# Two-layer attention and conv-FFN trunk on one core: gate and up products with the high and the low part of the tokens side by side in one 512 column operand

## The chip, the core and the metric

The kernel runs on one core of one Trainium2 chip. The metric is device microseconds of one execution, the median of three runs. The engines are named as the profile names them: PE (TensorE, matrix products; PEld is its load of the stationary operand), ACT (ScalarE), DVE (VectorE), POOL (GpSimd), and SP, whose queue issues the weight DMAs.

## What is computed

The reference is a decoder trunk of two layers over 256 tokens of width 1024: layer 0 mixes tokens by block attention (one block covers all 256 tokens here), layer 1 by differential attention. After each mixer comes the part that is changed here, a feed forward with a causal convolution of width 3 on its gate branch:

```python
def conv_ffn(x, w_in, conv_w, conv_b, w_out):
    h = x @ w_in                                             # (256, 1024) @ (1024, 2 * 2816)
    gate = causal_dwconv(h[..., :D_FF], conv_w, conv_b)      # 3 taps along the tokens
    return (jax.nn.silu(gate) * h[..., D_FF:]) @ w_out       # (256, 2816) @ (2816, 1024)

for i in range(DEPTH):                                       # DEPTH = 2
    h = h + mixer_i(rmsnorm(h, norm_mix_g[i]))
    h = h + conv_ffn(rmsnorm(h, norm_ffn_g[i]), ...)
```

All of it is float32. The kernel reaches that precision by splitting each factor of a product into a high part of type float32r and a low part, the rest, and summing three products: high by high, high by low, low by high.

## The kernel before

**Weights.** They come from HBM as 98 chunks of [128, 2048] (1 MB), in the order of their use, into the ring `raw` of 3 buffers. `split_next` (line 156) splits a chunk in two halves of 1024 columns: ACT copies the high part into `wh` (line 165), DVE subtracts to get the low part `wl` (line 167). Both have 5 buffers, so the split of chunk c + 5 waits until PE is through with chunk c. `split_upto` says how far the splits have got at each place of the program.

**Tokens.** The normalised activations lie with the features on the partitions in two tiles, `xh` (high) and `xl` (low), each [128, 2 token tiles, 8 contraction tiles, 128].

**Feed forward** (`ffn`, line 679). The 2816 hidden features go in 11 pairs of 128, j = 0 to 10. Each pair has three chunks: gate (u = 0), up (u = 1) and out (u = 2). Pair 0 is computed with the tokens on the partitions (`first_pair`) and turned by transposes (`turn`), since one tile of tokens is normalised before the other. Pairs 1 to 10 use `form_b` (line 697): for a gate or an up chunk, and for each of its two blocks b of 128 features, 3 x 8 products of 256 moving columns (all tokens) accumulate into one half of a PSUM bank:

```python
for ph in range(3):
    for k in range(KT):
        r.append(mm(p[:, b * 256:(b + 1) * 256], w[:, k, b], (xh, xh, xl)[ph][:, :, k], ...))
```

`post_gate` (line 710) takes the bank of the gate to SBUF: per block one ACT instruction with the last tap as scale and the bias (line 715), two DVE instructions for the other taps (line 717), and for the pair one Silu on ACT (line 719). `post_up` (line 722) multiplies that by the bank of the up product on DVE (line 724) and splits the result into a high part (ACT, line 726) and a low part (DVE, line 727) in the tile `arena`. `outp` (line 732) multiplies it by the out chunk, products of 512 columns into four accumulators `acc`.

**Order.** From the second pair on the loop asks, for j = 2 to 10, for gate(j), out(j - 2), up(j). After the last pair come out(9) and out(10), the sum with `h` and the next norm (`tail`, and `finish` at the end of the kernel). All PE work of 128 x 512 results uses two PSUM pools of four banks, `acc` and `wk`; `form_b`, the transposes and the scores use `wk`. The order of the instructions on ACT and DVE, and small moves on PE, are a scheduler's; the table `PLAN` places a few small works among the products (`turn`: after how many products the transposes of pair 0 stand).

In names such as wh22 the number is the chunk: 16 and 17 are gate and up of pair 0 in layer 0, 18 and 19 those of pair 1, 20 gate of pair 2, 21 out of pair 0, 22 up of pair 2, 23 gate of pair 3; 95 is up of pair 10 of layer 1, 96 and 97 are out of pairs 9 and 10.

Of the kernel before, what the change touches and what calls it, by code (L numbers as in the profile page):

```python
# [32 lines left out]

# the places of the small works among the products: slots of 24 products, or products
PLAN = {
# [21 lines left out]
    "norm_2": (42, 58),  # L57
    "turn": (21, 32),
}
# [3 lines left out]
def tile_trunk(  # L63
# [35 lines left out]

    # ---- inputs that come first  # L100
    h = [const.tile([128, D], F32, name=f"h{t}") for t in range(NT)]
# [21 lines left out]

    # ---- the stream of weight chunks, each split into two parts that sum to it
    raws, WH, WL = {}, {}, {}
# [23 lines left out]
    def after(engine):  # L149
        """the splits do not go before a chain that the products wait for"""  # L150
        return tc.issue_after(behind[engine].ins) if engine in behind else nullcontext()
# [21 lines left out]
    def split_upto(n):  # L173
        """n: pieces, two to a chunk (after the first)"""
        while state["split"] < min(n + 2, len(pieces)):
            split_next()

    def pump(c):
        """chunk c and those before it"""
        return [(PLAN["pump"][0], lambda: split_upto(2 * c + 1)), (PLAN["pump"][1], lambda: split_upto(2 * c + 2))]  # L180
# [37 lines left out]

    # ---- normalised activations, transposed and split
    xh = const.tile([128, NT, KT, 128], F32R, name="xh")  # L220
    xl = const.tile([128, NT, KT, 128], F32R, name="xl")
    st = {}
# [7 lines left out]
    def stats(t, i):  # L230
        """sum of squares over half i of the columns of h[t]"""
        junk = work.tile([128, D], F32, name="junk", bufs=1)[:, cols(i)]
        return nc.scalar.activation(junk, h[t][:, cols(i)], AF.Square, scale=1.0 / 32.0,
                             accum_out=st[t][1][:, i:i + 1])
# [30 lines left out]
    def gain_t(t, i, layer, parts=((0, 1, 2, 3),)):  # L265
        """without the scale of the norm, which the products get"""
        for ks in parts:
# [13 lines left out]

    # ---- matrix products: lists of single instructions, so that others go between
    def mm(o, l, r, start, stop):
# [3 lines left out]
    def passes(n, lh, ll, rh, rl):  # L287
        """(k, left, right) over the three products of parts"""
        return ([(k, lh, rh) for k in range(n)] + [(k, lh, rl) for k in range(n)]
                + [(k, ll, rh) for k in range(n)])  # L290

    def run(main, smalls=(), unit=1):
        """write down the products, with the small works at their places among them"""
        n = len(main)
        at = {}
        for pos, f in smalls:
            at.setdefault(min(pos * unit, n), []).append(f)
        for i in range(n + 1):
            for f in at.get(i, []):
                f()  # L300
            if i < n:
                main[i]()

    def proj(o, c0, t):
        """[128 tokens, 512] of the projection whose weights are chunks c0, c0 + 1"""
        r = []
        for c in (c0, c0 + 1):
            for k in (0, 2):
                r += proj_part(o, c, 4 * (c - c0), k, t, c == c0 and k == 0, c > c0 and k == 2)
        return r  # L310

    def proj_part(o, c, kt, k0, t, first, last):
        """the part of proj that comes from two rows of tiles of one chunk"""
        r = []
# [7 lines left out]

    # ---- attention
    def mixer(layer, base):
# [16 lines left out]
        def tables():  # L341
            """the rotary tables, times the scale of the norm"""
            p = wk()
# [6 lines left out]
        def evac_qk(p, kind, hf, j):  # L350
            """two heads, features on the partitions"""
            if j == 0:
# [132 lines left out]

        # where the small works go: (slot of 24 products, place in it)
        def ev(time, f, *a):
# [14 lines left out]

        # projections
        def form_b(o, c0, hl):
            """[128 features of a head, 256 tokens]"""
            r = []
# [76 lines left out]

        # the projection of the output
        b = base + 12
# [21 lines left out]
    def tail(m0, m1, po, gi=None):  # L607
        """the last products of a part, the sum with h and the norm that follows"""
        mix = gi is None
# [21 lines left out]
    def finish(outp, po, gi):  # L631
        """the last products, the sum with h and the last norm"""
        def products(t, n, *where):
# [43 lines left out]

    # ---- feed forward
    def ffn(layer, base):
# [16 lines left out]

        def form_b(j, u):
            p = wk()
            c = chunk_of[j, u]
            r = []  # L700
            for b in range(2):
                for ph in range(3):
                    for k in range(KT):
                        w = (WH, WL, WH)[ph][c].rearrange("p (k b f) -> p k b f", k=KT, b=2)
                        r.append(mm(p[:, b * 256:(b + 1) * 256], w[:, k, b],
                                    (xh, xh, xl)[ph][:, :, k],
                                    ph == 0 and k == 0, ph == 2 and k == KT - 1))
            return p, r

        def post_gate(j, p):  # L710
# [11 lines left out]
        def post_up(j, p):  # L722
            y = G[j]
            nc.vector.tensor_tensor(y, y, p.rearrange("p (b q) -> p b q", b=2), op=ALU.mult)  # L724
            g = arena([2, 2, 256], F32R)
            nc.scalar.copy(g[:, 0], y)  # L726
            nc.vector.tensor_tensor(g[:, 1], y, g[:, 0].bitcast(F32), op=ALU.subtract)
            G[j] = g
# [3 lines left out]
        def outp(j, t, n, o=None, off=0):  # L732
            """the part of pair j in [128 tokens, 512], or in 256 of its columns"""
            g = G[j]
# [15 lines left out]

        # the first pair with tokens on the partitions: one tile of them is ready before the other
        tok = {}
# [24 lines left out]
        split_upto(2 * (base + 5) + 2)  # L777
        p, r = form_b(1, 0)

        def both():  # L780
            turn(1)
            post_gate(0, pg)
            post_up(0, pu)

        run(r, [(PLAN["turn"][1], both)])
        post_gate(1, p)
        split_upto(2 * (base + 6) + 2)
        p, r = form_b(1, 1)
        run(r)
        post_up(1, p)  # L790
        for t in range(2):
            for n in range(2):
                po[t, n] = acc()
        for j in range(2, NP):
            for u in range(2):
                split_upto(2 * (chunk_of[j, u] + 3) + 2)
                p, r = form_b(j, u)
                run(r)
                (post_gate if u == 0 else post_up)(j, p)
                if u == 0:  # L800
# [12 lines left out]

    # ---- the whole
    fixed = tc.manual_schedule()
# [18 lines left out]
def ffn_order():  # L834
    """the order in which the feed forward asks for its chunks: (pair, gate | up | out)"""
    seq = [(0, 0), (0, 1), (1, 0), (1, 1)]
# [78 lines left out]
```

## Time and profile before

| | |
|---|---|
| median of 3 runs | 623.27 us (621.47 to 624.48) |
| profiled execution: span from the first to the last instruction | 620.5 us |
| median less that span (what lies around the instructions) | 2.8 us |
| mean granted TensorE clock | 0.997 |
| PE busy | 609.2 us, 98% |
| DVE, ACT busy | 410.3 us (66%), 345.6 us (56%) |
| HBM read | 104.58 MB, 170 GB/s over the span |

The profile gives no separate device time for the profiled execution; its span is what the sum is made against, and 2.8 us is added to compare with the median. A busy PE is not PE at its peak, since matmuls overlap; how long a product takes of PE is read from the distance between the starts of products that follow each other. Small groups of rows are merged: "x8" behind a row of the timeline says that eight like instructions stand in it.

### The profile page before, as it was taken

The numbers are of one execution on the slowest core, as the hardware profiler recorded it, in microseconds if no ns is written. First come the engines' busy times: TensorE is split into PE (matmuls) and PEld (weight loads), VectorE is DVE, ScalarE is ACT, GpSimd is POOL, SyncE is SP. The second block draws the span as 40 slices with busy tenths as digits, with TensorE's granted clock in tenths as the row PEclk, the third lists the DMA queues.
The fourth block names the chain that finished last, engine by engine and source line by source line (L and its number), as shares of the span: only waits on it lengthen the run. The fifth ranks groups of instructions, "written<-read, shape, count | busy, mean of one in ns | idle before, by whom it ended". The sixth has DMA issues, their size and how long they took to land.

```text
span 620.5 us, 10285 instructions
## 1 busy us (share of the span) xinstructions
PE 609.2 (98%) x4203; PEld 561.6 (91%) x4203; DVE 410.3 (66%) x676; ACT 345.6 (56%) x560; POOL 18.6 (3%) x29
## 2 busy tenths in 40 slices
PE   7999999999999999999999999999999999999996
PEld 5999988899999999999889998889999999999985
DVE  3799684587655665566575899965876566556624
ACT  5777574276454455445477798744755544444512
POOL 1100000000000000000010001011000000000000
PEclk9999999999999999999999999999999999999998
DMA  8686345165555455545353612450765545545101
GB/s 286 213 308 240 139 153 203 69 229 198 185 204 175 169 200 204 173 171 200 136 196 116 232 69 77 170 209 22 271 213 194 184 164 195 203 163 182 65 0 69
DMA packets 16756, 106.28 MB, mean 171 GB/s; under 512 B 2115, under 2 KB 2627, under 8 KB 4422
## 3 DMA queue, kind: packets, MB, share of 16 engines
q1 hardware_dynamic: 16422, 105.24, 47.8%
q8 instruction: 33, 0.54, 0.4%
q10 hardware_dynamic: 288, 0.39, 0.2%
q14 instruction: 13, 0.11, 0.0%
HBM read 104.58 MB, written 1.05 MB: 170 GB/s over the span
## 4 chain that ended last, share of the span: by engine, by line
PE 88%; ACT 5%; DMA 2%; DVE 2%; issue 1%; SPq 0%; POOL 0%; POOLq 0%; ACTq 0%
PE acc L284 46%; PE wk L284 37%; DMA raw<-in_wts_dram 2%; PE wk L383 2%; ACT swap L360 2%; ACT wh L165 1%; ACT sc L398 1%; DVE wl L167 1%; PE wk L424 1%; PE wk L257 1%; PE wk L480 0%; DVE swap L363 0%; DVE arena L364 0%; PE wk L443 0%; PE wk L442 0%
## 5 line engine op out<-in xcount | busy, mean ns | idle before, releaser
L167 DVE TENSOR_TENSOR wl<-raw,wh 128x1024 fp32r<-128x1024 f32 (+1 forms) x198 | 236.1, 1220 | 62.1 <-ACT wh L165 62.1
L165 ACT CAST wh<-raw 128x1024 fp32r<-128x1024 f32 (+1 forms) x198 | 198.2, 1040 | 94.3 <-PE wk L284 63.5
L284 PE MATMUL acc<-wh,arena 128*128 128x512 f32 x472 | 132.1, 397 | 0.0
L284 PEld LDWEIGHTS acc<-wh,arena 128*128 128x128 f32 x472 | 86.9, 188 | 19.4 <-ACT arena L726 0.5
L284 PE MATMUL wk<-xh,wl 128*128 128x256 f32 x640 | 90.0, 283 | 0.0
L284 PE MATMUL wk<-xl,wh 128*128 128x256 f32 x640 | 89.8, 283 | 0.0
L284 PE MATMUL wk<-xh,wh 128*128 128x256 f32 x640 | 89.4, 282 | 0.0
L284 PEld LDWEIGHTS wk<-xh,wh 128*128 128x128 f32 x640 | 83.4, 191 | 1.6
L284 PEld LDWEIGHTS wk<-xl,wh 128*128 128x128 f32 x640 | 82.6, 192 | 0.0
L284 PEld LDWEIGHTS wk<-xh,wl 128*128 128x128 f32 x640 | 82.5, 192 | 0.0
L284 PE MATMUL acc<-wl,arena 128*128 128x512 f32 x236 | 73.0, 398 | 0.0
L717 DVE SCALAR_TENSOR_TENSOR qsb<-wk,conv,qsb 128x255 f32<-128x255 f32 (+1 forms) x88 | 41.7, 480 | 40.7 <-ACT qsb L715 39.3
L715 ACT ACTIVATE qsb<-wk,conv 128x256 f32<-128x256 f32 x44 | 24.7, 563 | 58.6 <-PE wk L284 57.2
L284 PEld LDWEIGHTS acc<-wl,arena 128*128 128x128 f32 x236 | 44.0, 188 | 10.3
L724 DVE TENSOR_TENSOR qsb<-qsb,wk 128x512 f32<-128x512 f32 x22 | 15.0, 687 | 45.2 <-PE wk L284 44.2
L284 PE MATMUL acc<-xh,wh 128*128 128x256 f32 x256 | 43.0, 286 | 0.1
L284 PE MATMUL acc<-xh,wl 128*128 128x256 f32 x256 | 43.1, 285 | 0.0
L284 PE MATMUL acc<-xl,wh 128*128 128x256 f32 x256 | 41.5, 284 | 0.0
L284 PEld LDWEIGHTS acc<-xh,wh 128*128 128x128 f32 x256 | 35.7, 191 | 0.6 <-ACT wh L165 0.3
L284 PEld LDWEIGHTS acc<-xh,wl 128*128 128x128 f32 x256 | 35.7, 191 | 0.1
L284 PEld LDWEIGHTS acc<-xl,wh 128*128 128x128 f32 x256 | 35.3, 191 | 0.1
L360 ACT COPY swap<-acc 8x512 f32<-8x512 f32 (+1 forms) x48 | 27.7, 578 | 10.9 <-PE acc L284 8.8
(109 smaller groups left out, 553.5 us busy)
## 6 DMA issues: line engine op xcount, KB each, us to landing
raw<-in_wts_dram SPq DMA_DIRECT2D x96, 1024.0 KB, 4.8
h<-in_x_dram SPq DMA_DIRECT2D x4, 256.0 KB, 6.7
raw<-in_wts_dram SPq DMA_DIRECT2D x4, 256.0 KB, 6.1
raw<-in_wts_dram SPq DMA_DIRECT2D x2, 512.0 KB, 7.9
out_dram<-hn SPq DMA_DIRECT2D x2, 320.0 KB, 2.5
tab<-in_rope_dram SPq DMA_DIRECT2D x2, 256.0 KB, 6.8
out_dram<-hn ACTq DMA_DIRECT2D x2, 192.0 KB, 2.7
lamv<-in_lams_dram SPq DMA_DIRECT2D x1, 128.0 KB, 6.0
```

The lines of the kernel that those rows point to most:

```text
L165: nc.scalar.copy(hi, r)
L167: nc.vector.tensor_tensor(lo, r, hi.bitcast(F32), op=ALU.subtract)
L257: nc.tensor.transpose(p[:, k * 128:(k + 1) * 128], st[t][0][:, (4 * i + k) * 128:(4 * i + k + 1) * 128], ident)
L284: return lambda: nc.tensor.matmul(o, l() if callable(l) else l, r() if callable(r) else r, start=start, stop=stop)
L360: nc.scalar.copy(w[a:a + half], pv[b:b + half])
L383: nc.tensor.matmul(p[:, b * 128:(b + 1) * 128], q[r, hl, tq * 128:(tq + 1) * 128], k[r, hl, tk * 128:(tk + 1) * 128], start=True, stop=True)
L398: nc.scalar.activation(es[m][:, c], es[m][:, c], AF.Exp, bias=sm[:, 1, i:i + 1], scale=scale, accum_out=sm[:, 2, i:i + 1])
L424: nc.tensor.transpose(p[:, b * 128:(b + 1) * 128], es[0][:, b * 128:(b + 1) * 128], ident)
L715: nc.scalar.activation(y[:, b], pb, AF.Identity, bias=cw[:, 3:4], scale=cw[:, 2:3])
L717: nc.vector.scalar_tensor_tensor(y[:, b, s:], pb[:, :256 - s], cw[:, 2 - s:3 - s], y[:, b, s:], op0=ALU.mult, op1=ALU.add)
L724: nc.vector.tensor_tensor(y, y, p.rearrange("p (b q) -> p b q", b=2), op=ALU.mult)
```

## The change

Three things change, all in the feed forward's pairs 1 to 10 of both layers.

1. `xh` and `xl` become views of one tile `xx` [128, 8 contraction tiles, 2 parts, 2 token tiles, 128], so that for one contraction tile the high and the low part of all 256 tokens are 512 columns in a row.
2. `form_b` does one block of 128 features at a time, in a bank of its own. For each contraction tile there is one product of 512 columns (high weights by high and low tokens) and one of 256 columns (low weights by high tokens) that adds to the right half of the bank.
3. The two halves of the bank are summed on the way out (`summed`): ACT copies the left half to a tile `zg` or `zu`, DVE adds the right half. The convolution of the gate then reads that tile in SBUF, and its first tap goes from ACT to DVE. The product with the up branch waits for both blocks of `zu`.

The place of the second `turn` is now 16, the end of the first block.

```diff
-    "turn": (21, 32),
+    "turn": (21, 16),
...
-    xh = const.tile([128, NT, KT, 128], F32R, name="xh")
-    xl = const.tile([128, NT, KT, 128], F32R, name="xl")
+    xx = const.tile([128, KT, 2, NT, 128], F32R, name="xx")
+    xh = xx[:, :, 0].rearrange("p k t q -> p t k q")
+    xl = xx[:, :, 1].rearrange("p k t q -> p t k q")
...
-        def form_b(j, u):
+        def form_b(j, u, b):
             p = wk()
             c = chunk_of[j, u]
             r = []
-            for b in range(2):
-                for ph in range(3):
-                    for k in range(KT):
-                        w = (WH, WL, WH)[ph][c].rearrange("p (k b f) -> p k b f", k=KT, b=2)
-                        r.append(mm(p[:, b * 256:(b + 1) * 256], w[:, k, b],
-                                    (xh, xh, xl)[ph][:, :, k],
-                                    ph == 0 and k == 0, ph == 2 and k == KT - 1))
+            for k in range(KT):
+                hi, lo = (w[c].rearrange("p (k b f) -> p k b f", k=KT, b=2)[:, k, b] for w in (WH, WL))
+                r.append(mm(p, hi, xx[:, k].rearrange("p c t q -> p (c t q)"), k == 0, False))
+                r.append(mm(p[:, 256:], lo, xx[:, k, 0].rearrange("p t q -> p (t q)"), False, k == KT - 1))
             return p, r
+        def summed(name, b, p):
+            if b == 0:
+                parts[name] = work.tile([128, 2, 256], F32, name=name)
+            z = parts[name][:, b]
+            nc.scalar.copy(z, p[:, :256])
+            nc.vector.tensor_tensor(z, z, p[:, 256:], op=ALU.add)
+            return z
+        def gated(j, b, z):
+            if b == 0:
+                G[j] = work.tile([128, 2, 256], F32, name="qsb", bufs=3)
+            y = G[j]
+            cw = conv_t[:, layer, 2 * j + b]
+            nc.vector.tensor_scalar(y[:, b], z, cw[:, 2:3], cw[:, 3:4], op0=ALU.mult, op1=ALU.add)
+            for s in (1, 2):
+                nc.vector.scalar_tensor_tensor(y[:, b, s:], z[:, :256 - s], cw[:, 2 - s:3 - s],
+                                               y[:, b, s:], op0=ALU.mult, op1=ALU.add)
+            if b == 1:
+                nc.scalar.activation(y, y, AF.Silu)
+        def part_done(j, u, b, p):
+            z = summed(("zg", "zu")[u], b, p)
+            if u == 0:
+                gated(j, b, z)
+            elif b == 1:
+                post_up(j, parts["zu"])
...
-                p, r = form_b(j, u)
-                run(r)
-                (post_gate if u == 0 else post_up)(j, p)
+                for b in range(2):
+                    p, r = form_b(j, u, b)
+                    run(r)
+                    part_done(j, u, b, p)
```

Pair 0 keeps `post_gate` and its way through `turn`. The mixers' products are as before, but read the new tile.

How the instructions stand now, at the places that the prediction speaks of. **PE, one gate chunk** (names: result <- moving, stationary or the other way round; the number behind a tile's name is its buffer). Before, pair 3 of layer 0, both blocks into one bank:

```order
L284 MATMUL wk_2019<-xh_109,wh29_1853 128x256 x8
L284 MATMUL wk_2019<-xh_109,wl29_1854 128x256 x8
L284 MATMUL wk_2019<-xl_110,wh29_1853 128x256 x8
L284 MATMUL wk_2019<-xh_109,wh29_1853 128x256 x8
L284 MATMUL wk_2019<-xh_109,wl29_1854 128x256 x8
```

Now, the end of the second block of a gate chunk (pair 2) and the first products of the out chunk that follows:

```order
L285 MATMUL wk_1548<-xx_109,wh20_1323 128x512
L285 MATMUL wk_1548<-xx_109,wl20_1324 128x256
L285 MATMUL wk_1548<-xx_109,wh20_1323 128x512
L285 MATMUL wk_1548<-xx_109,wl20_1324 128x256
L285 MATMUL wk_1548<-xx_109,wh20_1323 128x512
L285 MATMUL wk_1548<-xx_109,wl20_1324 128x256
L285 MATMUL acc_1512<-wh21_1390,arena_1428 128x512 x2
```

The 24 products of a block, in three runs of 8, became 16 that change width and stationary operand at every step.

**ACT at the start of the first feed forward**, from the copy that leads to the second `turn`. Before:

```order
L771 COPY qsb_1389<-acc_1336 128x512
L165 CAST wh22_1472<-raw22_1322 128x1024 x2
L715 ACTIVATE qsb_1436<-wk_1332,conv_104 128x256
L715 ACTIVATE qsb_1464<-wk_1399,conv_104 128x256
L165 CAST wh23_1537<-raw23_1330 128x1024
L715 ACTIVATE qsb_1436<-wk_1332,conv_104 128x256
L715 ACTIVATE qsb_1464<-wk_1399,conv_104 128x256
```

Now:

```order
L801 COPY qsb_1388<-acc_1335 128x512
L165 CAST wh22_1461<-raw22_1321 128x1024
L745 ACTIVATE qsb_1419<-wk_1331,conv_104 128x256
L715 COPY zg_1431<-wk_1398 128x256
L165 CAST wh22_1461<-raw22_1321 128x1024
L165 CAST wh23_1516<-raw23_1329 128x1024
L745 ACTIVATE qsb_1419<-wk_1331,conv_104 128x256
L715 COPY zg_1431<-wk_1438 128x256
```

Pair 0's gate lies in the bank wk_1331 (before wk_1332); its second block's instruction (L745, before L715) stands behind the first half of chunk 23 in both, but that bank is now the next one that PE asks for: the second up block of pair 1 goes into it. DVE's share of the same stretch, now:

```order
L747 SCALAR_TENSOR_TENSOR qsb_1419<-wk_1331,conv_104,qsb_1419 128x255
L728 SCALAR_TENSOR_TENSOR qsb_1434<-zg_1431,conv_104,qsb_1434 128x255
L747 SCALAR_TENSOR_TENSOR qsb_1419<-wk_1331,conv_104,qsb_1419 128x254
L728 SCALAR_TENSOR_TENSOR qsb_1434<-zg_1431,conv_104,qsb_1434 128x254
L716 TENSOR_TENSOR zg_1431<-zg_1431,wk_1438 128x256
L716 TENSOR_TENSOR zu_1486<-zu_1486,wk_1469 128x256
```

The bank is free after the third of these rows.

**PE at the end of the last feed forward**, between the last up block and the first product of out(10), which needs the newest `arena`. Before there are 7 products of out(9) in between:

```order
L284 MATMUL acc_4554<-wh96_5820,arena_5817 128x512 x2
L284 MATMUL acc_4554<-wl96_5821,arena_5817 128x512 x2
L284 MATMUL acc_4554<-wh96_5820,arena_5817 128x512 x2
L284 MATMUL acc_4555<-wh96_5820,arena_5817 128x512
L284 MATMUL acc_4554<-wh97_5883,arena_5963 128x512 x2
```

Now there are 11:

```order
L285 MATMUL acc_4333<-wh96_5439,arena_5436 128x512 x2
L285 MATMUL acc_4333<-wl96_5440,arena_5436 128x512 x2
L285 MATMUL acc_4333<-wh96_5439,arena_5436 128x512 x2
L285 MATMUL acc_4334<-wh96_5439,arena_5436 128x512 x2
L285 MATMUL acc_4334<-wl96_5440,arena_5436 128x512 x2
L285 MATMUL acc_4334<-wh96_5439,arena_5436 128x512
L285 MATMUL acc_4333<-wh97_5492,arena_5562 128x512 x2
```

Four products of the next accumulator moved ahead of out(10).

## Rows read from the trace of the kernel before

**Rows 1.** The page's first part: busy time and share of the span

```profile
span 620.5 us, 10285 instructions
PE 609.2 (98%) x4203; PEld 561.6 (91%) x4203; DVE 410.3 (66%) x676; ACT 345.6 (56%) x560; POOL 18.6 (3%) x29
```

**Rows 2.** Busy time by stretch: one pair of layer 0, then both feed forwards

```profile
core 0: us, PE busy (x) PEld busy (x) DVE busy (x) ACT busy (x) POOL busy (x), PEclk, DMA share, GB/s
148.80:165.90 17.10, 17.10 (x123) 16.01 (x122) 10.15 (x12) 8.07 (x10) 0.00 (x0) 1.00 0.56 189
...
143.00:306.00 163.00, 163.00 (x1125) 151.35 (x1124) 97.91 (x118) 79.44 (x106) 0.55 (x1) 1.00 0.53 188
...
424.00:603.00 179.00, 178.97 (x1290) 168.91 (x1289) 108.67 (x133) 86.34 (x110) 2.38 (x2) 1.00 0.45 159
```

**Rows 3.** PE's timeline (start, duration): an up and a gate chunk, to out's start

```profile
205.68 1.10 PE L284 MATMUL wk<-xh,wh 128*128 128x256 f32 x8
206.62 1.12 PE L284 MATMUL wk<-xh,wl 128*128 128x256 f32 x8
...
217.17 0.40 PE L284 MATMUL acc<-wh,arena 128*128 128x512 f32 x1
```

**Rows 4.** Groups by line and shape: one of three like groups of form_b

```profile
L284 PE MATMUL wk<-xh,wl 128*128 128x256 f32 x640 | 90.0, 283 | 0.0
```

**Rows 5.** PE's timeline elsewhere: out(0), a value projection, finish's 256 column products

```profile
148.77 0.63 PE L284 MATMUL acc<-wh,arena 128*128 128x512 f32 x2
...
154.38 0.39 PE L284 MATMUL wk<-xh,wh 128*128 128x256 f32 x2
...
79.78 0.62 PE L284 MATMUL acc<-wh,xh 128*128 128x512 f32 x2
...
83.86 0.61 PE L284 MATMUL acc<-wh,xh 128*128 128x512 f32 x2
...
611.34 0.40 PE L284 MATMUL wk<-wh,arena 128*128 128x256 f32 x2
...
613.93 0.40 PE L284 MATMUL wk<-wh,arena 128*128 128x256 f32 x2
```

**Rows 6.** Groups by line and shape: ACT and DVE instructions that set prices

```profile
L715 ACT ACTIVATE qsb<-wk,conv 128x256 f32<-128x256 f32 x44 | 24.7, 563 | 58.6 <-PE wk L284 57.2 <-DVE qsb L717 1.4
...
L717 DVE SCALAR_TENSOR_TENSOR qsb<-wk,conv,qsb 128x255 f32<-128x255 f32 x44 | 20.9, 480 | 39.3 <-ACT qsb L715 39.3
...
L425 ACT COPY arena<-wk 128x384 f32<-128x384 f32 x16 | 7.5, 480 | 6.4 <-PE wk L424 6.3
...
L410 DVE TENSOR_SCALAR sc<-sc,smx 128x256 f32<-128x256 f32 x8 | 2.8, 344 | 0.0
...
L641 DVE TENSOR_TENSOR h<-wk,h 128x256 f32<-128x256 f32 x2 | 0.8, 422 | 0.2 <-PE wk L284 0.2
```

**Rows 7.** Timeline: start of pair 1 in layer 0 and in layer 1

```profile
131.07 1.12 PE L284 MATMUL wk<-xh,wh 128*128 128x256 f32 x8
...
133.59 2.00 ACT L165 CAST wh<-raw 128x1024 fp32r<-128x1024 f32 x2 [1.73 <-DMA raw<-in_wts_dram]
...
436.95 1.12 PE L284 MATMUL wk<-xh,wh 128*128 128x256 f32 x8
...
440.47 2.00 ACT L165 CAST wh<-raw 128x1024 fp32r<-128x1024 f32 x2 [2.72 <-DMA raw<-in_wts_dram]
440.80 0.60 PE L764 MATMUL wk<-ident,qsb 128*128 128x128 f32 x4
441.15 1.20 PE L284 MATMUL wk<-xh,wl 128*128 128x256 f32 x8
```

**Rows 8.** Timeline: from the last up product to out(10)

```profile
602.81 0.63 PE L284 MATMUL acc<-wh,arena 128*128 128x512 f32 x2
...
603.08 0.69 DVE L724 TENSOR_TENSOR qsb<-qsb,wk 128x512 f32<-128x512 f32 x1 [5.11 <-PE wk L284]
...
603.80 0.62 ACT L726 CAST arena<-qsb 128x512 fp32r<-128x512 f32 x1 [8.17 <-DVE qsb L724]
...
604.47 0.30 PEld L284 LDWEIGHTS acc<-wh,arena 128*128 128x128 f32 x2 [0.30 <-ACT arena L726]
```

More of the change, by code (lines that the diff above doesn't have):

```diff
@@ L700, in form_b @@
             r = []
-            for b in range(2):
-                for ph in range(3):
-                    for k in range(KT):
-                        w = (WH, WL, WH)[ph][c].rearrange("p (k b f) -> p k b f", k=KT, b=2)
-                        r.append(mm(p[:, b * 256:(b + 1) * 256], w[:, k, b],
-                                    (xh, xh, xl)[ph][:, :, k],
-                                    ph == 0 and k == 0, ph == 2 and k == KT - 1))
-            return p, r
+            for k in range(KT):
+                hi, lo = (w[c].rearrange("p (k b f) -> p k b f", k=KT, b=2)[:, k, b] for w in (WH, WL))
+                r.append(mm(p, hi, xx[:, k].rearrange("p c t q -> p (c t q)"), k == 0, False))
+                r.append(mm(p[:, 256:], lo, xx[:, k, 0].rearrange("p t q -> p (t q)"), False, k == KT - 1))
+            return p, r
+        def summed(name, b, p):
[5 more added lines that the diff above has]
+            return z
+        parts = {}
+        def gated(j, b, z):
[15 more added lines that the diff above has]
+                post_up(j, parts["zu"])
         def post_gate(j, p):
@@ L723, in post_up @@
             y = G[j]
-            nc.vector.tensor_tensor(y, y, p.rearrange("p (b q) -> p b q", b=2), op=ALU.mult)
+            nc.vector.tensor_tensor(y, y, p, op=ALU.mult)
             g = arena([2, 2, 256], F32R)
@@ L777, in ffn @@
         split_upto(2 * (base + 5) + 2)
-        p, r = form_b(1, 0)
         def both():
@@ L782, in both @@
             post_gate(0, pg)
-            post_up(0, pu)
+            post_up(0, pu.rearrange("p (b q) -> p b q", b=2))
+        p, r = form_b(1, 0, 0)
         run(r, [(PLAN["turn"][1], both)])
-        post_gate(1, p)
+        part_done(1, 0, 0, p)
+        p, r = form_b(1, 0, 1)
+        run(r)
+        part_done(1, 0, 1, p)
         split_upto(2 * (base + 6) + 2)
-        p, r = form_b(1, 1)
-        run(r)
-        post_up(1, p)
+        for b in range(2):
+            p, r = form_b(1, 1, b)
+            run(r)
+            part_done(1, 1, b, p)
         for t in range(2):
@@ L796, in ffn @@
                 split_upto(2 * (chunk_of[j, u] + 3) + 2)
-                p, r = form_b(j, u)
-                run(r)
-                (post_gate if u == 0 else post_up)(j, p)
+                for b in range(2):
+                    p, r = form_b(j, u, b)
+                    run(r)
+                    part_done(j, u, b, p)
                 if u == 0:
```

## Prediction

> **What bounds the kernel now.** I read the page's first part before anything else: PE is busy for 609.2 of 620.5 us, DVE for 66%, ACT for 56% [rows 1]. Since a share over the whole span mixes stages, the next view is the table by stretch. There the reader is to see that both feed forwards have PE busy without a break (163.00 of 163.00 us and 178.97 of 179.00), while one pair of 17.10 us asks DVE for 10.15 and ACT for 8.07 [rows 2]. So in the changed part the time is the number of products times the distance between their starts, and DVE and ACT matter only where PE comes to wait for them. The third view is PE's timeline, from which that distance is read, since the durations of single products overlap.
>
> **The products: the same columns in fewer instructions.** A block of 128 features is 24 products of 256 columns before, 6144 columns; after, 8 of 512 and 8 of 256, again 6144. Arithmetic is not removed. What goes is 8 products, each with its load of a stationary operand. The three groups of `form_b` have 640 products each [rows 4], so there are 1920/24 = 80 blocks, and 640 products less.
>
> The old price: from 205.68 to 217.17 us an up and a gate chunk run, four blocks, 96 products [rows 3]. That is 11.49/96 = 119.7 ns each, 2.873 us a block.
>
> The new price is 8 times a 512 column product and a 256 column one. I take 119.7 ns for the second. For the first the trace shows two: the 24 products of out(0) take 148.77 to 154.38, 233.8 ns each, and 18 products of a value projection take 79.78 to 83.86, 226.7 ns each [rows 5]. The out products lie in the same stage, but their stationary operand is the `arena`; the projection reads the token tile, though not as its moving operand as here. Neither is nearer, so I take the middle, 230 ns: 350 ns for the two, 2.80 us a block, 0.073 us saved, times 80 gives **5.8 us**. With 226.7 it would be 8.2, with 233.8 only 3.6; these are the ends of this term. At a change of width the old trace shows no extra: the first run of 256 column products after the 512s takes 205.68 to 206.62, 8 in 0.94 us, 117.5 ns each [rows 3].
>
> The Trainium skill, page "TensorE: Matmul & The Clock Gate", section "Back-to-back issue gap", gives a warm product N/2.4 + 2.5 ns, so an instruction saved would be worth 2.5 ns and the change, by an estimate from that page, 640 x 2.5 = 1.6 us; the sum would end at 622.9. The trace's 119.7 ns for 256 columns is above its 109.2, so the page does not describe this stream; what of it the rows bear out is the first rival.
>
> **The way out of PSUM.** It adds per block a copy on ACT and a sum on DVE, and moves the first tap from ACT to DVE. The copy of 128 x 256 has no row; it lies between nothing and the 480 ns of a 128 x 384 copy, and I take 0.4 us. The sum is priced by a DVE sum of 256 PSUM columns with SBUF, 422 ns, the tap by a 128 x 256 instruction of one tensor, 344 ns; the tap it replaces cost ACT 563 ns [rows 6]. Per pair DVE gets 4 x 0.422 + 2 x 0.344 = 2.4 us more, ACT 4 x 0.4 - 2 x 0.563 = 0.5. DVE then needs 12.5 and ACT 8.6 of some 16.8 us, so both stay under PE, and I cost this at nothing inside the loop. The cover is the ring of four `wk` banks: each block takes a bank of its own, so a bank comes round after two gate blocks, the out products and two up blocks, some 14 us after it was filled; the evacuation needs the copy and the sum, 0.8 us, and stands behind at most a split or two (2.00 us for two halves on ACT [rows 7]). The splits keep their lead too: chunk c + 5 is still asked for when c is done, four chunks before its use. New tile layouts move the same bytes; I cost them at nothing, the cover being the same.
>
> **Two places without that cover.** First, the start of pair 1. Banks now go twice as fast, so the second up block takes the bank in which pair 0's gate lies. Its release hangs on this queue of ACT: a half split, pair 0's first block, `zg`, a half split, then a half of chunk 23 (in layer 1: 72), which waits until PE is through with the gate chunk of pair 1, and only then pair 0's second block; behind it on DVE three instructions of 0.48 us [rows 6] until the bank is free. In layer 1 the gate chunk starts at 436.95 [rows 7]. Two blocks of 2.80 and the 0.35 us of transposes (440.80 to 441.15) end at 442.9, the next ends at 445.7, and there PE wants the bank. The split starts at 440.47, when its DMA has landed: by the queue 441.5, 442.0, 442.4, 443.4, after PE's release of the chunk (442.9 and some 0.3 for the last product to end, which lasts 283 ns [rows 4]); the next half goes to 444.4, the ACT instruction to 445.0, DVE to 446.4. PE waits 0.7 us. In layer 0 the chunk starts at 131.07 and the split at 133.59 [rows 7]; the wait for PE rules there (131.07 + 5.95 + 0.3 = 137.3), then 1.0 + 0.56 + 3 x 0.48 gives 140.3, against 139.8 asked: 0.5. Together **1.2 us** lost; the ends are nothing, if the queues run freer, and 3 us, if each wait is twice as long.
>
> Second, the end of the last feed forward. Out(10) needs the newest `arena`. Before, DVE starts the product with up 0.27 us after PE's first out product, and the loader is released at 604.47, 0.3 us late [rows 8]. Now the chain is 0.27 + 0.4 + 0.42 + 0.69 + 0.62 and some 0.05 at each handoff, 2.6 us. The cover grows from 7 to 11 products of 233.8 ns, 2.57 us. So I cost it at nothing, at most 0.3 either way; in layer 0 more products lie between.
>
> **Sum.** 620.5 - 5.8 + 1.2 = 615.9 us of span. The median of the runs lies 2.8 us above the span, so **618.7 us** against 623.27, 0.7% faster. About 0.5%, 3.1 us, is what a measurement of this kernel can tell from no change.
>
> **Rivals.**
> *Only a small fixed part goes with an instruction.* The last 256 column products, 22 from 611.34 to 613.93, take 117.7 ns each, the 512s of out 233.8 [rows 5]: doubled, 117.7 is but 1.6 above, so nearly all of the time goes with the columns. If the new stream behaves like these, 640 x 1.6 = 1.0 us are saved, and with the same 1.2 us lost it ends at 623.5, no change. For it: these two prices are from the stage of the change. Against it: in `form_b` itself a 256 column product costs 119.7, and 226.7 for 512 columns is seen. Chance 0.2. The 2.5 ns of the Trainium skill would end here too.
> *Slower: the alternation costs.* All rows of 512 and 256 column products are from runs of one width; the new stream changes width at each of its 1280 products, 640 of each, and the load for a 512 column product has only a 256 column one to hide behind. If each of the 1280 loses the 7 ns that lie between the two prices of 512 columns [rows 5], that is 9.0 us: 623.3 - 5.8 + 1.2 + 9.0 = 627.7. Over 3.6 ns a product the gain is gone, over 6.0 the kernel is 0.5% slower. Against it: the change of width in rows 3 is free, and loads run at that pace under 256 column products now. Chance 0.1.
> That the change doesn't do what it says is out: 640 products fewer stand in its program.
>
> **How the numbers follow.** Forecast 0.7, the first rival 0.2, the second 0.1. Within the forecast, term by term from 8.2 - 0 to 3.6 - 3, the gain passes 3.1 us in about five cases of six, 0.58 in all. Faster 0.58; same 0.12 + 0.2 = 0.32; slower 0.10. The range goes from 614.8 (8.2 saved and little lost: 623.3 - 8.2 = 615.1, and a little for the runs' spread) to 624.0, which takes in the first rival; the second stays outside.
>
> **What would show it.** In the new profile: a gate or up chunk at about 5.6 us from start to start instead of 5.75, pairs at 16.8 instead of 17.1; DVE near 12.5 us a pair; a wait of PE before the second up block of pair 1, of 0.4 to 1.2 us, and none in the loop. It is wrong if the 512 and 256 column products together take over 356 ns or under 345, or if PE waits for banks in every pair.

## Result and profile after: 0.8% faster

The changed kernel takes 617.15 us (median of six runs, 615.09 to 619.37) against 622.37 us of the kernel before, now also over six runs. The ratio is 0.9916, with a 95% interval of 0.9892 to 0.994: 5.2 us, between 3.7 and 6.7. The forecast was 618.7 us and "faster".

The page's first part, after [rows 1]:

```profile
span 616.6 us, 9112 instructions
PE 602.3 (98%) x3563; PEld 527.2 (86%) x3563; DVE 450.3 (73%) x796; ACT 352.6 (57%) x600; POOL 19.4 (3%) x29
```

PE has 640 instructions less and is still the bound. The table by stretch, for pair 1 of layer 0 (from its gate to out(0)), one pair of the loop, and pair 1 of layer 1 [rows 2]:

```profile
132.94:150.82 17.88, 17.55 (x103) 15.11 (x101) 15.59 (x26) 12.02 (x19) 0.00 (x0) 0.95 0.72 276
156.41:173.11 16.70, 16.70 (x90) 14.20 (x89) 13.19 (x21) 8.66 (x13) 0.00 (x0) 0.95 0.57 194
435.67:454.30 18.63, 17.84 (x103) 15.15 (x101) 16.55 (x27) 12.05 (x19) 0.00 (x0) 0.95 0.76 272
```

In the loop PE is never idle and a pair takes 16.70 instead of 17.10 us. At pair 1 PE is idle for 0.33 and 0.79 us. PE's timeline, an up and a gate chunk to out's start, which answers to rows 3:

```profile
206.49 0.40 PE L285 MATMUL wk<-xx,wh 128*128 128x512 f32 x1
206.73 0.27 PE L285 MATMUL wk<-xx,wl 128*128 128x256 f32 x1
206.84 0.40 PE L285 MATMUL wk<-xx,wh 128*128 128x512 f32 x1
...
217.59 0.62 PE L285 MATMUL acc<-wh,arena 128*128 128x512 f32 x2
```

Two chunks take 11.10 us instead of 11.49: 32 times a 512 and a 256 column product, 346.9 ns for the two, where three products of 119.7 ns took 359.1.

**Where the 3.9 us between the two profiled spans come from.** From the start of pair 1's gate to the start of out(9), layer 0 takes 162.57 us (132.94 to 295.51) instead of 165.84, layer 1 163.38 (435.67 to 599.05) instead of 165.86: 5.75 us less. The rest takes 1.85 us more, and nearly all of that (1.87) lies ahead of the first feed forward, which this execution reached at 132.94 instead of 131.07 us. The runs' medians differ by 5.2 us, near the 5.75. Whether the way to the first feed forward has become dearer is a question for an experiment (the layout, below).

**The waits at pair 1.** PE's waits, three of seven rows:

```profile
PE wk L384 <- DVE arena L365: 2.4, 1, 2.4
...
PE wk L285 <- DVE qsb L747: 0.6, 2, 0.3
PE wk L285 <- DVE zg L716: 0.5, 1, 0.5
```

The first of these lies in layer 0's mixer. The others lie at pair 1: the second for the last tap of pair 0's gate (once in each layer), the third for the sum of pair 1's first gate block. PE's timeline shows the two places of layer 1:

```profile
441.61 0.28 PE L285 MATMUL wk<-xx,wl 128*128 128x256 f32 x1
442.40 0.47 PE L285 MATMUL wk<-xx,wh 128*128 128x512 f32 x1 [0.51 <-DVE zg L716]
...
445.18 0.28 PE L285 MATMUL wk<-xx,wl 128*128 128x256 f32 x1
445.74 0.47 PE L285 MATMUL wk<-xx,wh 128*128 128x512 f32 x1 [0.28 <-DVE qsb L747]
```

The first up block starts at 442.40 and the second at 445.74. The same stretch on ACT:

```profile
439.23 1.05 ACT L165 CAST wh<-raw 128x1024 fp32r<-128x1024 f32 x1 [2.77 <-DMA raw<-in_wts_dram]
440.19 0.56 ACT L745 ACTIVATE qsb<-wk,conv 128x256 f32<-128x256 f32 x1
440.64 0.36 ACT L715 COPY zg<-wk 128x256 f32<-128x256 f32 x1
440.90 1.06 ACT L165 CAST wh<-raw 128x1024 fp32r<-128x1024 f32 x1
442.78 1.05 ACT L165 CAST wh<-raw 128x1024 fp32r<-128x1024 f32 x1 [0.82 <-DMA raw<-in_wts_dram]
443.74 0.55 ACT L745 ACTIVATE qsb<-wk,conv 128x256 f32<-128x256 f32 x1
```

and on DVE:

```profile
440.31 1.23 DVE L167 TENSOR_TENSOR wl<-raw,wh 128x1024 fp32r<-128x1024 f32 x1 [1.44 <-ACT wh L165]
441.45 0.48 DVE L747 SCALAR_TENSOR_TENSOR qsb<-wk,conv,qsb 128x255 f32<-128x255 f32 x1
441.85 0.41 DVE L716 TENSOR_TENSOR zg<-zg,wk 128x256 f32<-128x256 f32 x1
...
444.33 0.48 DVE L747 SCALAR_TENSOR_TENSOR qsb<-wk,conv,qsb 128x255 f32<-128x255 f32 x1 [0.22 <-ACT qsb L745]
444.73 0.47 DVE L728 SCALAR_TENSOR_TENSOR qsb<-zg,conv,qsb 128x255 f32<-128x255 f32 x1
445.12 0.48 DVE L747 SCALAR_TENSOR_TENSOR qsb<-wk,conv,qsb 128x254 f32<-128x254 f32 x1
```

This is the chain of the forecast: half a split, pair 0's first block behind it, half a split of the next chunk, pair 0's second block, three DVE instructions, and 445.74 on PE. Only the split of the next chunk waits for something else than forecast: its DMA, until 442.78, not PE, which was through with the gate chunk by 441.9 (441.61 and the 0.28 of its last product). In layer 0 the two come almost together: the gate chunk's last product ends at 139.16, and the split starts at 139.30, again put down to its DMA:

```profile
139.30 1.06 ACT L165 CAST wh<-raw 128x1024 fp32r<-128x1024 f32 x1 [1.10 <-DMA raw<-in_wts_dram]
```

The first up block of layer 1 waits for another instruction, the sum of pair 1's first gate block (441.85 to 442.26 on DVE). Its copy was there at 441.00, but on DVE half a split (until 441.54) and pair 0's first tap stand ahead of it.

**The end.** The last out product, which answers to rows 8, on PE's loader:

```profile
601.50 0.30 PEld L285 LDWEIGHTS acc<-wh,arena 128*128 128x128 f32 x2 [0.17 <-ACT arena L756]
```

The loader is 0.17 us late, which the products running at that time cover; before it was 0.30.

### The profile page after: what moved, and what is told of

It is laid out like the page before. It is cut to its first block, busy times and chain, and to the rows that moved or that the text cites. A ratio compares the mean times of both kernels' runs of the same rounds, so it can differ in the third digit from the quotient of the medians.

```text
span 616.6 us, 9112 instructions
## 1 busy us (share of the span) xinstructions
PE 602.3 (98%) x3563; PEld 527.2 (86%) x3563; DVE 450.3 (73%) x796; ACT 352.6 (57%) x600; POOL 19.4 (3%) x29
## 4 chain that ended last, share of the span: by engine, by line
PE 81%; ACT 7%; DVE 4%; DMA 4%; issue 2%; POOL 0%; SPq 0%; POOLq 0%; ACTq 0%
PE acc L285 42%; PE wk L285 33%; DMA raw<-in_wts_dram 4%; DVE wl L167 3%; ACT wh L165 2%; PE wk L384 2%; ACT swap L361 2%; ACT sc L399 1%; PE wk L271 1%; PE wk L425 1%; PE wk L258 0%; DVE arena L363 0%; PE wk L481 0%; DVE swap L364 0%; DVE arena L365 0%
## 5 line engine op out<-in xcount | busy, mean ns | idle before, releaser
L285 PE MATMUL wk<-xx,wh 128*128 128x512 f32 x640 | 223.9, 394 | 1.1 <-DVE qsb L747 0.6
L285 PE MATMUL wk<-xx,wl 128*128 128x256 f32 x640 | 178.4, 279 | 0.0
L285 PEld LDWEIGHTS wk<-xx,wh 128*128 128x128 f32 x640 | 119.9, 187 | 29.2 <-ACT wh L165 1.2
L285 PEld LDWEIGHTS wk<-xx,wl 128*128 128x128 f32 x640 | 120.6, 188 | 0.9
L285 PE MATMUL acc<-xx,wh 128*128 128x256 f32 x512 | 75.3, 285 | 0.1
L285 PEld LDWEIGHTS acc<-xx,wh 128*128 128x128 f32 x512 | 67.0, 191 | 0.7 <-ACT wh L165 0.3
L285 PE MATMUL acc<-wh,xx 128*128 128x512 f32 (+1 forms) x256 | 57.7, 350 | 2.2 <-ACT xx L274 2.1
L285 PEld LDWEIGHTS acc<-wh,xx 128*128 128x128 f32 x256 | 41.0, 193 | 8.5 <-ACT xx L274 2.5
L285 PE MATMUL acc<-xx,wl 128*128 128x256 f32 x256 | 43.1, 285 | 0.0
L728 DVE SCALAR_TENSOR_TENSOR qsb<-zg,conv,qsb 128x255 f32<-128x255 f32 x80 | 38.5, 482 | 1.7
L715 ACT COPY zu<-wk 128x256 f32<-128x256 f32 x40 | 14.8, 370 | 18.9 <-PE wk L285 18.9
```

What stands on the lines that cost most here:

```text
L285: return lambda: nc.tensor.matmul(o, l() if callable(l) else l, r() if callable(r) else r, start=start, stop=stop)
L715: nc.scalar.copy(z, p[:, :256])
L728: nc.vector.scalar_tensor_tensor(y[:, b, s:], z[:, :256 - s], cw[:, 2 - s:3 - s], y[:, b, s:], op0=ALU.mult, op1=ALU.add)
```

## Experiments

The theory: a product costs its columns and a fixed part, so that fewer and wider products save the fixed part 640 times; the way out of PSUM is hidden behind PE except at pair 1, where the ring of banks comes round before pair 0 has left it. The rivals: the gain comes from something else in the change; the alternation costs or saves; the evacuation costs. All times of this table are in us. The third to sixth columns are worked out from the starts of products in each trace: pair 1 from its gate to out(0) in layer 0 and layer 1; eight pairs of the loop in layer 0, up(2) to up(10); both stretches from pair 1's gate to out(9); and when pair 1 is reached in layer 0.

| kernel | median | pair 1 | eight pairs | both stretches | pair 1 reached at |
|---|---|---|---|---|---|
| before | 622.37 | 17.70, 17.72 | 136.80 | 331.70 | 131.07 |
| changed | 617.15 | 17.88, 18.63 | 133.55 | 325.95 | 132.94 |
| 512 split in two (e1) | 621.41 | 17.70, 18.52 | 136.80 | 332.50 | 130.59 |
| runs of eight (e2) | 616.85 | 17.85, 19.30 | 134.08 | 327.65 | 129.35 |
| pair 0 copied (e3) | 613.75 | 17.40, 17.40 | 133.60 | 324.30 | 132.08 |
| all 512 (e4) | 684.82 | 22.25, 22.70 | 161.07 | 392.84 | 132.31 |
| layout alone (e5) | 621.14 | 17.70, 17.71 | 136.80 | 331.69 | 131.33 |
| e3, more on DVE (e6) | 614.68 | 17.40, 17.40 | 133.60 | 324.24 | 130.79 |
| e3, no copy and sum (e7) | 616.88 | 18.09, 18.78 | 133.54 | 326.33 | 132.89 |
| e3, out by tile (e8) | 613.77 | 17.41, 17.40 | 133.54 | 324.20 | 129.74 |

The kernel before took 621.64 us in the runs beside e1 to e4, and 620.97 beside e5 to e8. The all 512 kernel was timed once.

### The wide product cut in two (e1)

```diff
-                r.append(mm(p, hi, xx[:, k].rearrange("p c t q -> p (c t q)"), k == 0, False))
-                r.append(mm(p[:, 256:], lo, xx[:, k, 0].rearrange("p t q -> p (t q)"), False, k == KT - 1))
+                xk = [xx[:, k, c].rearrange("p t q -> p (t q)") for c in range(2)]
+                r.append(mm(p[:, :256], hi, xk[0], k == 0, False))
+                r.append(mm(p[:, 256:], hi, xk[1], False, False))
+                r.append(mm(p[:, 256:], lo, xk[0], False, k == KT - 1))
```

> The 512 column product of a block is cut back into two of 256 (high weights by high tokens into the left half, by low tokens into the right half); banks, copy, sum and convolution stay as in the changed kernel. Theory (the gain is the 640 products saved, some 12 to 13 ns each): a block takes 24 x 119.7 ns = 2.87 us again instead of 2.77, a pair 17.1 us instead of 16.7, and 80 x 0.1 = 8 us come back: about 625, so slightly slower than the kernel before because the evacuation's waits at pair 1 stay. Rival (the gain lies in the new banks, order or evacuation, not in the number of products): it stays near 617.

Measured: 621.41 us, 0.9999 of the kernel before (0.998 to 1.0018). PE's timeline, from an up chunk to the out products:

```profile
205.19 0.39 PE L285 MATMUL wk<-xx,wh 128*128 128x256 f32 x2
...
216.69 0.63 PE L285 MATMUL acc<-wh,arena 128*128 128x512 f32 x2
```

96 products in 11.50 us, 119.8 ns each, although banks, copies and sums are those of the changed kernel. The eight pairs take 136.80 us, to the hundredth what they took before. So the gain of the loop is the number of products, and the rival falls. The forecast of 625 was too high. Both stretches give back 6.55 us, not 8, since pair 1 loses only 0.8 us in this version; the medians differ by only 4.26 us, and the rest of that lies outside the two stretches (the profiled execution reached pair 1 at 130.59 us, that of the changed kernel at 132.94).

### The same products in runs of eight (e2)

```diff
-            r = []
+            r, r2 = [], []
...
-                r.append(mm(p[:, 256:], lo, xx[:, k, 0].rearrange("p t q -> p (t q)"), False, k == KT - 1))
+                r2.append(mm(p[:, 256:], lo, xx[:, k, 0].rearrange("p t q -> p (t q)"), False, k == KT - 1))
+            r += r2
```

> Same products as the changed kernel, but in each block the eight of 512 columns first, then the eight of 256; nothing else. Theory (columns at 2.4 GHz plus some 13 ns a product, whatever its neighbour): 8 x 226.7 + 8 x 120 = 2.774 us a block, the same as now (346.7 a pair), 617 within 1 us. Rival (a change of width or of operand costs or saves something at each step): if the steps cost 7 ns each a block gets 0.1 us shorter and the kernel 8 us faster; if a 512 product in a run takes 233.8 as in the out products, a block is 0.06 longer and the kernel 4 to 5 us slower.

Measured: 616.85 us, 0.9922 of before (0.9899 to 0.9946). PE's timeline, four blocks:

```profile
203.09 1.99 PE L285 MATMUL wk<-xx,wh 128*128 128x512 f32 x8
204.91 1.11 PE L285 MATMUL wk<-xx,wl 128*128 128x256 f32 x8
205.86 2.00 PE L285 MATMUL wk<-xx,wh 128*128 128x512 f32 x8
207.70 1.11 PE L285 MATMUL wk<-xx,wl 128*128 128x256 f32 x8
208.66 2.00 PE L285 MATMUL wk<-xx,wh 128*128 128x512 f32 x8
...
214.24 0.63 PE L285 MATMUL acc<-wh,arena 128*128 128x512 f32 x2
```

A block takes 2.80 us (205.86 to 208.66) against 2.77 alternating. Changing width and operand at every product costs nothing that runs would give back; the runs are even 0.5 us dearer over eight pairs. The rival in which each step costs 7 ns falls; the one with 233.8 ns for each 512 column product does too, since eight of them take 1.84 us, 230 ns each. In layer 1 its pair 1 is longer, 19.30 us: PE waits 0.66 and 0.96 us there, where the changed kernel waits 0.51 and 0.28. In this execution the split that stands ahead of pair 0's second block got its DMA 7.89 us after the start of pair 1 (432.70), against 7.11 us in the changed kernel:

```profile
440.59 1.05 ACT L165 CAST wh<-raw 128x1024 fp32r<-128x1024 f32 x1 [1.49 <-DMA raw<-in_wts_dram]
```

Why that DMA came later is open.

### Both products at 512 columns (e4)

```diff
-                r.append(mm(p, hi, xx[:, k].rearrange("p c t q -> p (c t q)"), k == 0, False))
-                r.append(mm(p[:, 256:], lo, xx[:, k, 0].rearrange("p t q -> p (t q)"), False, k == KT - 1))
+                xk = xx[:, k].rearrange("p c t q -> p (c t q)")
+                r.append(mm(p, hi, xk, k == 0, False))
+                r.append(mm(p, lo, xk, False, k == KT - 1))
```

> Both products of a contraction tile take 512 columns (low weights by high and low tokens as well, so the product of the two low parts is added); 16 products of 512 in a block. It prices a 512 column product with the token tile as moving operand. Theory (213.3 ns of columns plus 13): 226.7 ns each, 3.63 us a block, 0.85 us more than now, 80 x 0.85 = 68 us more, about 685. Rival (512 column products of this place take 233.8 as the out products, and the 347 ns of a pair come from cheap 256 column ones beside them): 3.74 us a block, 694.

Measured: 684.82 us in one run. From PE's timeline, inside a block:

```profile
224.44 0.39 PE L285 MATMUL wk<-xx,wl 128*128 128x512 f32 x1
...
227.16 0.39 PE L285 MATMUL wk<-xx,wl 128*128 128x512 f32 x1
```

Twelve products in 2.72 us: 226.7 ns. Of the two prices of rows 5, that of the value projection holds here. With 120 ns for a 256 column product (119.8 in e1) it adds up to the loop's price of a pair of products, 346.7 ns; in the loop itself the starts are 230 and 117 ns apart, the same sum.

### Pair 0's gate copied out of its bank (e3)

```diff
+            z = work.tile([128, 2, 256], F32, name="zg")
+            nc.scalar.copy(z, p.rearrange("p (b q) -> p b q", b=2))
...
-                pb = p[:, b * 256:(b + 1) * 256]
-                nc.scalar.activation(y[:, b], pb, AF.Identity, bias=cw[:, 3:4], scale=cw[:, 2:3])
+                pb = z[:, b]
+                nc.vector.tensor_scalar(y[:, b], pb, cw[:, 2:3], cw[:, 3:4], op0=ALU.mult, op1=ALU.add)
```

> Pair 0's gate leaves its PSUM bank by one ACT copy of 128x512 to SBUF, and its taps then run on DVE from SBUF; all else as in the changed kernel. Theory (PE waits 0.33 us in layer 0 and 0.33 of the 0.79 us in layer 1 for the last tap of pair 0's gate, and after a stall the product stream of that pair runs at 353 instead of 347 ns for 512+256): the waits for the tap vanish, the stretch from pair 1's gate to out(0) falls from 17.9 and 18.6 to 17.2 and 17.5 to 18.2, total 1 to 1.5 us faster than 617. Rival (the bank is late because ACT's queue is late behind a split that waits for its DMA): the waits stay, now for the copy, and the time stays.

Measured: 613.75 us, 0.9875 of before (0.9847 to 0.9903). The table by stretch, pair 1 of layer 0 and of layer 1:

```profile
132.08:149.48 17.40, 17.40 (x102) 15.14 (x101) 15.24 (x27) 11.97 (x19) 0.00 (x0) 1.00 0.65 231
434.35:451.75 17.40, 17.40 (x102) 15.16 (x101) 15.29 (x26) 11.31 (x18) 0.00 (x0) 1.00 0.58 226
```

PE is no longer idle in either. Pair 1 falls by 0.48 and 1.23 us, 1.71 together: that is what the waits cost in the changed kernel, though the waits themselves add up to only 1.12 (0.33, 0.51 and 0.28). Most of the difference lies in PE's way in and out of a stall: at 441.61 to 442.40 and 445.18 to 445.74 above, the products stand 0.79 and 0.56 us apart instead of 0.12. ACT's split still waits for its DMA in this version:

```profile
438.00 1.05 ACT L165 CAST wh<-raw 128x1024 fp32r<-128x1024 f32 x1 [2.86 <-DMA raw<-in_wts_dram]
438.96 0.58 ACT L743 COPY zg<-wk 128x512 f32<-128x512 f32 x1
```

but one copy behind it now frees the whole bank at 439.5, where the last tap freed it at 445.6. That the first split waits for its DMA is thus not what decides; what stood between it and the last tap, a second split and the taps themselves, was. The other wait of layer 1, for the sum of pair 1's first gate block, went as well, which the theory had left between 17.5 and 18.2. One part of the theory fell: it put the 353 ns for two products down to the stalls and expected 17.2 us in layer 0, but pair 1 keeps 353 ns here without any stall, and takes 17.40.

This is the fastest version of the study. Its median is 3.4 us below that of the changed kernel (2.7 us when each is taken against the kernel before in the runs beside it), more than the 1 to 1.5 us of the theory. The trace gives 1.65 us of that in both stretches; the rest lies outside them and is not explained by the copy.

### The layout alone (e5)

```diff
-    xh = const.tile([128, NT, KT, 128], F32R, name="xh")
-    xl = const.tile([128, NT, KT, 128], F32R, name="xl")
+    xx = const.tile([128, KT, 2, NT, 128], F32R, name="xx")
+    xh = xx[:, :, 0].rearrange("p k t q -> p t k q")
+    xl = xx[:, :, 1].rearrange("p k t q -> p t k q")
```

> The kernel before with the token tiles as two views of one tile, and nothing else of the change. It asks whether the layout has a price of its own outside the feed forwards: the changed kernel reached pair 1 of layer 0 at 132.94 us, 1.87 us later than before, its wait for the rotated keys being 2.4 instead of 1.0 us. Theory (the way to the first feed forward differs from execution to execution with the arrival of the first weights; the layout costs nothing): the same time as before within 0.3%, pairs of 17.10 us, pair 1 reached at some 129 to 133 us. Rival (writing or reading the strided views is slower): pair 1 reached at 132.9 or later, some 1.9 us more in each execution, about 624.3.

Measured: 621.14 us, 1.0005 of before (0.9988 to 1.0022). PE's waits, the row for the rotated keys:

```profile
PE wk L384 <- DVE arena L365: 2.6, 1, 2.6
```

The wait is as long as in the changed kernel, yet pair 1 is reached at 131.33 us; and in e2, which has the same layout, this wait is missing from the list. Over the ten traces, one execution of each kernel, pair 1 is reached at 129.35 to 132.94 us, 3.6 us apart. With medians that agree within 0.2 us, the layout has no price that these runs can tell.

### More work for DVE, and less (e6, e7)

Both on top of the version with pair 0 copied. More:

```diff
+    extra = const.tile([128, 256], F32, name="extra")
...
             nc.vector.tensor_tensor(z, z, p[:, 256:], op=ALU.add)
+            for i in range(2):
+                nc.vector.tensor_tensor(extra, z, z, op=ALU.add)
```

> The kernel with pair 0's gate copied out, with two further DVE sums of 128x256 behind each block's own (results unused), 8 per pair of some 0.4 us: DVE goes from 12.2 to some 15.5 of 16.7 us a pair. It asks how much cover the evacuation has. Theory (DVE is hidden as long as it has less to do than PE; bank ring and split lead cover the order): pairs stay at 16.70 us, time within 1 us of 613.8. Rival (the cover is thin, since DVE's queue is in order and the splits of the weights stand behind the sums): PE waits for weights or banks in every pair; at 0.5 us a pair 10 us more, about 624.

Less, with the copy and the sum gone (`halves` is the second part of `post_up`, the split into `arena`):

```diff
-            z = summed(("zg", "zu")[u], b, p)
+            if u == 0:
+                gated(j, b, p[:, 256:])
+            else:
+                y = G[j]
+                nc.vector.tensor_tensor(y[:, b], y[:, b], p[:, 256:], op=ALU.mult)
+                if b == 1:
+                    halves(j)
+            return
...
+            halves(j)
+
+        def halves(j):
+            y = G[j]
```

> The kernel with pair 0's gate copied out, without the ACT copy and the DVE sum: the right half of each bank goes on alone, so the product of the two high parts is left out of gate and up in pairs 1 to 10. It prices the way out of PSUM that the change added: DVE falls by some 1.7 us a pair, ACT by 1.5. Theory (the evacuation is hidden behind PE): the same 613.8 within 1 us, pairs 16.70 us. Rival (copy and sum cost PE time through PSUM or the queues): pairs below 16.70 us, total 2 us or more faster.

Measured: 614.68 us (0.9889 of before, 0.9863 to 0.9915) and 616.88 us (0.9928, 0.9901 to 0.9954). The table by stretch, eight pairs' length of the loop, with more:

```profile
155.00:288.60 133.60, 133.60 (x705) 114.36 (x705) 121.75 (x214) 68.25 (x98) 0.00 (x0) 1.00 0.54 197
```

with less:

```profile
155.00:288.60 133.60, 133.60 (x706) 113.55 (x705) 90.75 (x122) 57.23 (x64) 0.00 (x0) 1.00 0.54 197
```

and with neither (e3):

```profile
155.07:288.67 133.60, 133.60 (x705) 114.37 (x704) 98.91 (x146) 67.58 (x97) 0.00 (x0) 1.00 0.55 198
```

DVE is busy for 121.75 of 133.60 us in the first, 90.75 in the second and 98.91 in the third; PE is busy throughout, and eight pairs take 133.60, 133.54 and 133.60 us. In the loop the way out costs nothing, with DVE 91% busy too. In the second DVE has 1.0 us less to do a pair, where 1.7 was expected; the reading does not hang on that.

Without the copy and the sum the kernel is even slower than e3, which neither theory had: at pair 1 PE waits 0.4 and 1.3 us for taps (18.09 and 18.78 us). In layer 1:

```profile
446.18 0.50 PE L285 MATMUL wk<-xx,wh 128*128 128x512 f32 x1 [1.26 <-DVE qsb L728]
```

Line 728 has the taps of pair 1's own gate blocks. They now read the banks themselves and hold them until the last tap, where the copy and the sum gave them back earlier.

### The out products by contraction tile (e8)

```diff
-            for ph in range(3):
-                for k in range(2):
+            for k in range(2):
+                for ph in range(3):
```

> The kernel with pair 0's gate copied out; in the out products the three products of one contraction tile follow each other (loops of phase and contraction tile swapped). It asks why a 512 column product takes 233.5 ns there and 226.7 with the token tile. Theory (it goes with the operand in the arena or its place, not with the order): 233.5 stays, 613.8. Rival (it goes with which products follow each other): 226.7, 24 x 6.8 = 0.16 us less a pair, 22 pairs 3.6 us faster, about 610.

Measured: 613.77 us, 0.9884 of before (0.9859 to 0.991). In this trace 24 out products take 5.60 us (147.15 to 152.75), 233.3 ns each, as before. The order of these products is not why they are dearer than 226.7. What the reason is stays open; no run with another operand there was made.

## Why the prediction was right

**PE as the bound, and the price of a product.** Right in its mechanism, with one size off. The forecast took 350 ns for a 512 and a 256 column product, in the middle between 346.7 and 353.8; the loop shows 346.7, the lower end. The 68 blocks outside pair 1 (32 in the loop and 2 of up(10) in each layer) gained 3.25 + 3.20 + 0.18 + 0.18 = 6.81 us, where 68 x 0.073 = 5.0 was forecast. The term that was off is "Neither is nearer, so I take the middle": the all 512 kernel shows 226.7 with the token tile as the moving operand. The caution was not idle, though: in pair 1 of the version without waits (e3) the same two products take 353 ns. PE's starts there are 232, 118, 240, 120, 236 and 114 ns apart, over and over, and 230 and 117 in the loop.

**The bank wait at pair 1.** Right place, the right chain in the main, too small: 1.2 us forecast, 1.71 measured (changed kernel less e3). In layer 0 the wait is 0.33 against 0.5; in layer 1 the second up block waits 0.28 against 0.7, but half a microsecond had already been lost at the first up block, for a sum that the forecast did not consider: it stands on DVE behind half a split and pair 0's first tap. The forecast also had the split of the next chunk wait for PE, where its DMA came last, by 0.14 us in layer 0 and 0.89 in layer 1. And the stalls cost more than PE's idle time.

**The way out.** Right. DVE needs 12.15 to 13.19 us a pair (12.5 forecast), ACT 8.5 to 8.7 (8.6). The prices, by line and shape over the loop of the changed kernel:

```profile
L715 ACT COPY zu<-wk 128x256 f32<-128x256 f32 x16 | 5.9, 370 | 5.3 <-PE wk L285 5.3
...
L716 DVE TENSOR_TENSOR zg<-zg,wk 128x256 f32<-128x256 f32 x16 | 6.6, 415 | 0.0
...
L726 DVE TENSOR_SCALAR qsb<-zg,conv 128x256 f32<-128x256 f32 x16 | 6.6, 410 | 0.3
```

The sum (415 ns) was taken at 422, the tap (410) at 344, the copy (370) at 400. That the cover is real is shown by e6 and e7.

**The end of the last feed forward.** Right: nothing lost.

**The sum.** 5.8 less 1.2 was to be 4.6 us; the two stretches gave 5.75. That this is so near is in part luck, since both terms were too small and the errors work against each other. At the loop's price, 6.81/68 = 0.10 us a block, all 80 blocks would have given 8.0 us; pair 1 fell 2.3 us short of that, 1.71 for the waits and the rest for its 353 ns. The 2.8 us between span and median were too many: the changed kernel's profiled run took 618.5 us with a span of 616.6, so 1.9 us lie around it, and the 620.5 of before with 1.9 is the 622.4 of its six runs. With 1.9 the forecast would have been 617.8. So a gain 1.15 us too small and an allowance 0.9 us too large point the same way, to a time above the measured 617.15.

**The rivals.** The first, that an instruction saved is worth 1.6 ns, is excluded: 6.81 us for 8 x 68 = 544 products is 12.5 ns each, and e1 takes the gain of the loop back by adding the products alone. The Trainium skill's page "TensorE: Matmul & The Clock Gate", section "Back-to-back issue gap", gives 2.5 ns beside the columns for a product that stands alone, a condition that the forecast left out; in this stream, where each product has its own load, 226.7 - 512/2.4 and 120 - 256/2.4 both leave some 13.3 ns, and the measurement decides. The second, that the alternation costs 7 ns a product, is excluded by e2 for the loop. In pair 1 two products take 6.6 ns more than in the loop, 3.3 each; that the alternation is what costs there is not shown.

## What to carry to other kernels

Where PE is never idle, price a product by the distance between starts in the very stream that is changed: here some 13 ns go with each product of 256 or 512 columns besides its columns, so a 512 column operand pays where it replaces two of 256 with the same stationary operand. Whether the 13 ns belong to the product or to its load of a stationary operand is open: every version here has one load for each product (PE and PEld show the same count in [rows 1] and in the page after). When each block takes a bank of its own, the ring comes round sooner: look at the first pair, where the longest evacuation stands behind splits and DMAs, and free that bank by one copy. An evacuation beside a busy PE cost nothing here, with its engine up to 91% full; where it begins to cost was not measured.

## What the runs showed of the hardware that was not expected

- The profiled run of the changed kernel shows a granted TensorE clock of 0.95 in every stretch read between 20 us and the end of the last feed forward, that of e3 1.00, both near the upper of the two levels, 2.4 GHz; a pair of the loop takes 16.70 us in both, and products stand as far apart. The other five runs of the changed kernel have a mean of 0.995 to 0.999 and take 615.09 to 619.37 us, the profiled one 618.50. A mean of 0.95 said nothing of the time here.
- The same alternating stream settles at one of two paces, 346.7 or 353 ns for two products, and keeps it until something comes between, such as another kind of product, the transposes or a stall: 346.7 after the out products in every pair of the loop, 353 after the first pair's products of 256 columns. In e3 the transposes left it at 353, in the changed kernel they brought 346.7. What chooses the pace is open, and no run was made for it.
- After a run of products with another width, 512 column products settle from the sixth on: in e2 they stand 233, 236, 228, 233, 231, 226, 227 and 227 ns apart. Eight of them take 27 ns more than 8 x 226.7, about the 20 to 30 ns by which a block of runs is dearer than an alternating one.
